# First modulation as columns: weight blocks held stationary, tokens turned in pairs, loads interleaved with the weights

## The chip, the core and the metric

The kernel runs on one core of a Trainium2 chip. The metric is device time in microseconds (us) of one launch. Engines are named as in the profile: PE is the matrix engine (PEld its weight loads), DVE the vector engine, ACT the scalar engine, POOL the GpSimd engine, SP the engine whose queue issues most DMAs. A matmul has a *stationary* operand, which a weight load puts into PE's array, and a *moving* operand, which is then streamed through it column by column.

## The reference, cut to what matters

One layer of a diffusion backbone with 1024 latent and 256 context tokens of width 1024. The part that the change touches is the first modulation, which everything else reads:

```python
mod_l = silu(c) @ w_ada + b_ada          # c: (1, 1024); w_ada: (1024, 6144)
mod_c = silu(c_ctx) @ w_ada + b_ada      # the context tokens have a vector of their own
sh1, sc1, g1, sh2, sc2, g2 = split(mod_l, 6)
hl = rmsnorm(x,   norm1_w) * (1 + sc1)  + sh1      # 8 tiles of 128 tokens
hc = rmsnorm(ctx, norm1_w) * (1 + csc1) + csh1     # 2 tiles of 128 tokens
y  = token_mix(hc, hl, ...)              # in-projection, 8 heads of mLSTM and retention, out-projection
xl = x + g1 * y
out = rmsnorm(xl + g2 * expert_choice_ffn(rmsnorm(xl) * (1 + sc2) + sh2))
```

All of it is float32. Of `w_ada`, the first 2048 columns (shift and scale, 8 MB) are needed before any projection can start.

## The kernel before, in words

The precise products go as two or three passes of a float32 form that PE takes in one pass each (`F32R`): a value is split into `hi` and `lo = value - hi`, and `hi*hi + hi*lo + lo*hi` is summed. A plain float32 matmul stands in the trace as two passes.

**The start.** `ccol` (both condition vectors, 8 blocks of 128 rows by 2) gives `sig = silu(ccol)`. The 8 MB of `w_ada` come as eight tiles `wa` of 1 MB (three buffers, line 222). Each of the four blocks of 512 modulation columns takes two tiles. In blocks 0 and 2 the kernel multiplies in plain float32 (line 271): `sig` (2 columns) is stationary, the weights move, 512 columns at a time. In blocks 1 and 3 the weights are first split by ACT and DVE (lines 275, 276), and the passes go in `F32R` (line 278), with a stationary tile `cst` of 128 columns. The result is a row of 512 values for both vectors in PSUM (`prow`); ACT copies it out (line 282) and four small matmuls (line 284) turn it into columns of `mps`, 128 partitions by 2.

**The tokens.** `norm_x` squares a tile of 128 tokens (ACT or DVE, lines 239, 237), POOL makes the inverse root (lines 128, 129) and DVE (tiles 0 to 5) or POOL (tiles 6 to 9, line 245) scales it. Then for each of three groups (context: tiles 0, 1; latent: 2 to 5; 6 to 9) and each of 8 blocks of 128 features, PE transposes the block of each token tile into `pt` (line 328), ACT applies scale and shift (`full`, line 330) and DVE makes `hh` and `hl` of it (lines 331, 332). Before them `b1` and `a1` (lines 302 to 304) are made of `mps`.

**The first head.** Its in-projection weights come as two tiles of 1 MB in the buffers of `wa`, are split by ACT and by DVE and POOL in turn (lines 179, 180), and `gemm` (line 355) multiplies `hh` and `hl` of a token tile with them, 24 passes for each tile. `gates` (lines 382, 387) does the same with 16 gate columns. `prep` makes keys, values and states of a token tile.

**Order.** The DMAs of the start are pinned in program order on SP's queue. On the other engines the recording layer orders instructions; each engine works through its own list in order, and an instruction that waits holds up what stands behind it on that engine. A tile's buffer comes free when its last reader is done. After the start come eight heads, the out-projection with the router, and sixteen experts whose weights stream from memory. The start is the only place that the change touches.

Of the kernel before, what the change touches and what calls it, by code (L numbers as in the profile page):

```python
# [71 lines left out]
def _pack(i):  # L72
# [15 lines left out]
    o["wada1"] = cont(wa[:, :2 * D].reshape(2, 4, 128, 4, 512).transpose(3, 0, 2, 1, 4))  # L88
# [30 lines left out]
def build(tc, A, out):  # L119
# [95 lines left out]

    early = ExitStack()
    ep = early.enter_context(tc.tile_pool(name="early", bufs=1))
    eps_ = early.enter_context(tc.tile_pool(name="early_ps", bufs=1, space=PSUM))
# [5 lines left out]
    def load_x(tt):  # L224
        if tt == 8:
            xts[8], xts[9] = (lambda a: (a[:, 0], a[:, 1]))(
                ep.tile([128, 4, 512], F32, name="wa", bufs=3).rearrange("p (a b) c -> p a (b c)", a=2))
        xt = xts[tt] if tt >= 8 else ep.tile([128, D], F32, name="xt", bufs=6)
        pinned(xt, A["ctx"][tt] if tt < NTC else A["x"][tt - NTC])
        xts[tt] = xt  # L230

    def norm_x(tt):
        xt = xts[tt]
        sq = ep.tile([128, D], BF16, name="sq")
        ss = ep.tile([128, 1], F32, name="ss", bufs=3)
        if tt % 2 and tt > 2:
            V.scalar_tensor_tensor(sq, xt, 1.0, xt, op0=ALU.mult, op1=ALU.mult, accum_out=ss)
        else:
            S.activation(sq, xt, AF.Square, accum_out=ss)
        r = ep.tile([128, 1], F32, name="r", bufs=3)  # L240
        rsqrt_mean(r, ss, D, ep)
        if tt < 6:
            V.tensor_scalar(xt, xt, r, None, op0=ALU.mult)
        else:
            G.tensor_scalar(xt, xt, r, 1.0, op0=ALU.mult, op1=ALU.mult)
# [7 lines left out]
    cst = ep.tile([128, 4 * KD + 128], F32R, name="cst")  # L253
    cs4 = cst[:, 0:4 * KD].rearrange("p (k s j) -> p k s j", s=2, j=2)
    V.tensor_copy(cst[:, 4 * KD:], ident)
    V.tensor_copy(cs4[:, :, :, 0], sig)
    V.tensor_tensor(cs4[:, :, :, 1], sig, cs4[:, :, :, 0].bitcast(F32), op=ALU.subtract)
    sel = ep.tile([4, 2], F32, name="sel")
    V.tensor_tensor(sel, ident[0:4, 0:4:2], ident[0:4, 1:4:2], op=ALU.add)

    ret_decay()
    mps = eps_.tile([128, 16, 2], F32, name="mps")
    for b in range(4):
        prow = eps_.tile([128, 512], F32, name="prow", bufs=2)
        for g in range(2):
            wa = ep.tile([128, 4, 512], F32, name="wa", bufs=3)
            pinned(wa, A["wada1"][b, g])
            for j in range(4):
                k = 4 * g + j
                if b % 2 == 0:  # L270
                    PE.matmul(prow[0:2], lhsT=sig[:, k], rhs=wa[:, j], start=(k == 0), stop=(k == 7))  # L271
                    continue
                wh = wp.tile([128, 512], F32R, name="whi")
                wl = wp.tile([128, 512], F32R, name="wlo")
                S.copy(wh, wa[:, j])
                V.tensor_tensor(wl, wa[:, j], wh.bitcast(F32), op=ALU.subtract)
                for q, w in enumerate((wh, wl)):
                    PE.matmul(prow, lhsT=cst[:, 4 * k:4 * k + 128], rhs=w, start=(k == 0 and q == 0),
                              stop=(k == 7 and q == 1))
        nr = 2 if b % 2 == 0 else 4  # L280
        rows = ep.tile([128, 512], F32, name="full", bufs=3)[0:nr]
        S.copy(rows, prow[0:nr])
        for j in range(4):
            PE.matmul(mps[:, 4 * b + j], lhsT=rows[:, j * 128:(j + 1) * 128],
                      rhs=sel if nr == 4 else ident[0:2, 0:2], start=True, stop=True)
    for tt in groups[0]:
        load_x(tt)
        norm_x(tt)
    wcur = [], []
    for q in range(2):  # L290
        wa = ep.tile([128, 4, 512], F32, name="wa", bufs=3)
        pinned(wa.rearrange("p (a b) c -> p a b c", a=2),
               A["win"][HEADS[0], 2 * q:2 * q + 2].rearrange("a p b c -> p a b c"))
        for j in range(4):
            split_w(wa[:, j], wcur, G if j % 2 else V)
    for tt in groups[1]:
        load_x(tt)
        norm_x(tt)
# [8 lines left out]
    pinned(wg, A["wmg"])  # L307
    wgt = cp.tile([128, 32 * KD + 96], F32R, name="wgs")
    wgs = wgt[:, 0:32 * KD].rearrange("p (k c) -> p k c", k=KD)
    for tt in groups[2]:  # L310
        load_x(tt)
    first = [pinned(kpre, A["k_pre"])]
# [5 lines left out]
    for gi, grp in enumerate(groups):  # L318
        if gi == 2:
            for tt in grp:  # L320
                norm_x(tt)
        n = 128 * len(grp)
        hh, hl = hT[gi]
        w = 1 if gi == 0 else 0
        for k in range(KD):
            pt = eps_.tile([128, 512], F32, name="pt", bufs=3)
            for j, tt in enumerate(grp):
                PE.transpose(pt[:, j * 128:(j + 1) * 128], xts[tt][:, k * 128:(k + 1) * 128], ident)
            full = ep.tile([128, 512], F32, name="full", bufs=3)
            S.activation(full[:, :n], pt[:, :n], AF.Identity, bias=b1[:, k, w:w + 1], scale=a1[:, k, w:w + 1])  # L330
            V.tensor_copy(hh[:, k], full[:, :n])  # L331
# [996 lines left out]
```

## Time and profile before

| | us |
|---|---|
| three runs: median (lowest to highest) | 2330.57 (2322.81 to 2331.26) |
| the profiled execution | 2328.49 |
| its span, first to last instruction | 2326.7 |
| first pass on PE | 8.48 |
| `mps` complete (36.39 + 1.05) | 37.44 |
| first pass of the in-projection | 41.55 |
| in-projection of the fourth token tile starts | 77.25 |
| PE gets over its wait for the first `qk` | 86.95 |

The mean granted clock of PE over the span is 0.987 of full speed; full is 2.4 GHz, half is 1.2 GHz. The start that the change touches is the first 4% of the span.

How to read the rows below: a line of a timeline is *start, duration, engine, line, operation, out<-in, shapes, count, [idle before it <- what ended that]*, with several equal instructions in one line. For PE, `128*2 128x512` is stationary partitions and columns, then moving partitions by columns. Durations on PE run from a pass's start to its end and overlap with the next pass; the distance from one start to the next is what a pass costs in a stream.

### The profile page before, as it was taken

What the parts mean: (1) busy time and instruction counts of PE and PEld (TensorE: products, weight loads), DVE (VectorE), ACT (ScalarE), POOL (GpSimd) and SP (SyncE); (2) the same over time, 40 slices, a digit from 0 to 9 for tenths busy, and PEclk for the clock granted to TensorE, in tenths of its full rate; (3) what the DMA queues carried; (4) which work ended last, traced back from release to release, by engine and by line L of the source; (5) the groups of instructions that cost most, each with busy time, mean ns of one, the idle gap of its engine ahead of it and who ended that gap; (6) DMA issues with size and microseconds to landing.
All of it is one profiled execution on the core that took longest, in us unless ns stands there. A gap on an engine that the chain in (4) does not pass through costs nothing.

```text
span 2326.7 us, 31080 instructions
## 1 busy us (share of the span) xinstructions
PE 2255.3 (97%) x11270; PEld 1851.0 (80%) x11270; DVE 1788.6 (77%) x2092; ACT 1415.9 (61%) x1812; POOL 385.4 (17%) x724
## 2 busy tenths in 40 slices
PE   7999999999997899999999999999999999999997
PEld 4788888888786677888888888888888888888886
DVE  5554545655556989888888888988888889888887
ACT  5433434222434566777777677677776777777775
POOL 2444445444411000000000000000000000000004
PEclk8999999999998999999999999999999999999999
DMA  7123322233474879999999999999999999999995
GB/s 283 53 60 105 109 71 81 87 107 127 136 270 168 323 287 348 365 380 380 362 383 357 381 376 363 382 366 376 375 364 381 365 375 374 364 387 357 376 396 230
DMA packets 133390, 664.68 MB, mean 286 GB/s; under 512 B 14221, under 2 KB 44021, under 8 KB 64629
## 3 DMA queue, kind: packets, MB, share of 16 engines
q1 hardware_dynamic: 126181, 635.78, 72.2%
q0 software_dynamic: 6768, 24.83, 3.8%
q8 instruction: 88, 1.44, 0.2%
q10 hardware_dynamic: 288, 2.10, 0.2%
q14 instruction: 65, 0.53, 0.1%
HBM read 637.50 MB, written 25.15 MB: 285 GB/s over the span
## 4 chain that ended last, share of the span: by engine, by line
PE 82%; DMA 6%; DVE 5%; ACT 2%; issue 2%; POOL 2%; SPq 0%; POOLq 0%; ACTq 0%; DVEq 0%
PE w_gate L976 20%; PE w_up L976 20%; PE y L976 20%; PE g L355 10%; DMA raw<-in_wada 3%; PE y L741 3%; PE T L976 3%; DVE lo L976 2%; DMA raw<-in_win 1%; PE U L573 1%; PE prow L271 1%; POOL r L129 1%; DVE raw L668 1%; ACT hi L976 1%; PE O L621 1%
## 5 line engine op out<-in xcount | busy, mean ns | idle before, releaser
L976 DVE TENSOR_TENSOR lo<-raw,hi 128x2048 fp32r<-128x2048 f32 x528 | 1185.2, 2286 | 134.5 <-ACT hi L976 122.3
L976 ACT CAST hi<-raw 128x2048 fp32r<-128x2048 f32 x528 | 971.6, 1903 | 0.9 <-DVE xl L976 0.6
L976 PE MATMUL w_gate<-hi,xh 128*128 128x512 f32 (+1 forms) x768 | 298.7, 389 | 0.1
L976 PE MATMUL w_gate<-hi,xl 128*128 128x512 f32 (+1 forms) x768 | 291.3, 379 | 0.0
L976 PE MATMUL w_gate<-lo,xh 128*128 128x512 f32 (+1 forms) x768 | 290.5, 378 | 0.0
L976 PE MATMUL w_up<-hi,xl 128*128 128x512 f32 (+1 forms) x768 | 289.6, 377 | 0.0
L976 PE MATMUL w_up<-lo,xh 128*128 128x512 f32 (+1 forms) x768 | 288.9, 376 | 0.5 <-DVE lo L976 0.5
L976 PE MATMUL w_up<-hi,xh 128*128 128x512 f32 (+1 forms) x768 | 288.4, 376 | 0.0
L976 ACT CAST th<-T 128x512 fp32r<-128x512 f32 x96 | 53.0, 552 | 330.8 <-PE T L976 330.8
L355 PE MATMUL g<-whi,hh 128*128 128x512 f32 (+1 forms) x640 | 248.2, 388 | 4.0 <-DVE hh L331 2.1
L355 PE MATMUL g<-whi,hl 128*128 128x512 f32 (+1 forms) x640 | 246.0, 384 | 1.3 <-DVE hl L332 1.2
L355 PE MATMUL g<-wlo,hh 128*128 128x512 f32 (+1 forms) x640 | 243.6, 381 | 0.0
L976 PE MATMUL y<-lo,th 128*128 128x512 f32 x704 | 226.6, 395 | 0.7 <-DVE lo L976 0.7
L976 PE MATMUL y<-hi,th 128*128 128x512 f32 x704 | 226.8, 396 | 0.5 <-ACT th L976 0.5
L976 PE MATMUL y<-hi,tl 128*128 128x512 f32 x704 | 226.2, 395 | 0.0
L1227 POOL DMA_INDIRECT acc_d<-yo,idx x15 | 23.8, 1588 | 889.2 <-DVE yo L976 889.2
L976 PEld LDWEIGHTS w_gate<-hi,xl 128*128 128x128 f32 x768 | 145.4, 189 | 29.2
L976 PEld LDWEIGHTS w_up<-lo,xh 128*128 128x128 f32 x768 | 144.1, 188 | 30.8 <-DVE lo L976 1.1
L976 PEld LDWEIGHTS w_up<-hi,xh 128*128 128x128 f32 x768 | 144.5, 188 | 28.7
L976 PEld LDWEIGHTS w_gate<-lo,xh 128*128 128x128 f32 x768 | 145.8, 190 | 26.5
L976 PEld LDWEIGHTS w_up<-hi,xl 128*128 128x128 f32 x768 | 144.2, 188 | 28.4
L976 PEld LDWEIGHTS w_gate<-hi,xh 128*128 128x128 f32 x768 | 145.8, 190 | 26.2 <-ACT xh L976 0.5
(376 smaller groups left out, 3196.9 us busy)
## 6 DMA issues: line engine op xcount, KB each, us to landing
raw<-in_w_up SPq DMA_DIRECT2D x176, 1024.0 KB, 7.3
raw<-in_w_down SPq DMA_DIRECT2D x176, 1024.0 KB, 7.2
raw<-in_w_gate SPq DMA_DIRECT2D x174, 1024.0 KB, 7.2
raw<-in_wada SPq DMA_DIRECT2D x32, 512.0 KB, 4.4
raw<-in_win SPq DMA_DIRECT2D x28, 512.0 KB, 3.7
wa<-in_wada SPq DMA_DIRECT2D x8, 1024.0 KB, 4.9
xt<-in_x SPq DMA_DIRECT2D x14, 512.0 KB, 7.8
aux<-in_k_rope SPq DMA_DIRECT2D x32, 128.0 KB, 2.1
```

Of the source, the lines that this page charges most:

```text
L129: G.tensor_tensor(dst, m, mhalf, op=ALU.pow)
L271: PE.matmul(prow[0:2], lhsT=sig[:, k], rhs=wa[:, j], start=(k == 0), stop=(k == 7))
L355: PE.matmul(dst, lhsT=a[:, k], rhs=w[:, c0:512], start=(k == 0 and q == 0), stop=(k == 7 and q == 2))
L573: PE.matmul(pU[:, dr], lhsT=kw[:, dr], rhs=v[:, 0:NV], start=True, stop=True)
L621: PE.matmul(pO[:, dr], lhsT=k1[:, dr], rhs=v, start=True, stop=True)
L668: V.scalar_tensor_tensor(raw, raw, 1.0, crow, op0=ALU.mult, op1=ALU.mult, accum_out=mcol[:, n:n + 1])
L741: PE.matmul(y, lhsT=a[:, k], rhs=w[:, k], start=(k == 0 and q == 0), stop=(k == 7 and q == 2))
L976: return lambda *a, **k: tc.keep_in_program_order(f(*a, **k))
L1227: nc.gpsimd.indirect_dma_start(out=acc_d, out_offset=bass.IndirectOffsetOnAxis(ap=idx[:, :1], axis=0), in_=yo, in_offset=None, compute_op= ...
```

## The change

The modulation is now computed straight as columns. `w_ada` is packed into eight tiles of 256 modulation columns, each with the full depth of 1024 rows. For every 128 of these columns the weight block is the stationary operand (128 by 128, plain float32) and `sig` (2 columns) moves; eight such matmuls sum one column block of `mps`. `prow`, the split of `w_ada`, `cst`, `sel`, the copies and the turning are gone.

The loads are reordered on SP: the context tokens stand behind the sixth tile of weights, and the four quarters of the first head's weights around the eighth, each in a buffer of its own (`raw`, two buffers). Seven buffers `xt` hold token tiles. All splits of the first head go to DVE, and all ten scalings of tokens too (POOL keeps the inverse root).

The tokens are turned two tiles at a time instead of four: for each pair and each two feature blocks, four transposes into one PSUM tile (`O` and `I` in turn), two ACT instructions of 256 columns, one cast `hh` of 512 columns (DVE and ACT in turn) and one subtraction on DVE. The PSUM pools of the later stage are opened before the start and the start uses their tiles.

```diff
-    o["wada1"] = cont(wa[:, :2 * D].reshape(2, 4, 128, 4, 512).transpose(3, 0, 2, 1, 4))
+    o["wada1"] = cont(wa[:, :2 * D].reshape(KD, 128, 8, 256).transpose(2, 1, 0, 3).reshape(8, 128, 2048))
...
-        if tt < 6:
-            V.tensor_scalar(xt, xt, r, None, op0=ALU.mult)
-        else:
-            G.tensor_scalar(xt, xt, r, 1.0, op0=ALU.mult, op1=ALU.mult)
+        V.tensor_scalar(xt, xt, r, None, op0=ALU.mult)
...
-    mps = eps_.tile([128, 16, 2], F32, name="mps")
-    for b in range(4):
-        prow = eps_.tile([128, 512], F32, name="prow", bufs=2)
-        for g in range(2):
-            wa = ep.tile([128, 4, 512], F32, name="wa", bufs=3)
-            pinned(wa, A["wada1"][b, g])
-            for j in range(4):
-                k = 4 * g + j
-                if b % 2 == 0:
-                    PE.matmul(prow[0:2], lhsT=sig[:, k], rhs=wa[:, j], start=(k == 0), stop=(k == 7))
-                    continue
...
+    mps = psu.tile([128, 16, 2], F32, name="S")
+    raws = []
+    for t in range(8):
+        wa = ep.tile([128, KD, 256], F32, name="wa", bufs=3)
+        pinned(wa, A["wada1"][t].rearrange("p (k c) -> p k c", k=KD))
+        for c in range(2):
+            for k in range(KD):
+                PE.matmul(mps[:, 2 * t + c], lhsT=wa[:, k, c * 128:(c + 1) * 128], rhs=sig[:, k],
+                          start=(k == 0), stop=(k == 7))
+        if t == 5:
+            for tt in (0, 1):
+                load_x(tt)
+                norm_x(tt)
+        if t >= 6:
+            for q in (2 * t - 12, 2 * t - 11):
+                raws.append(wp.tile([128, 2, 512], F32, name="raw", bufs=2))
+                pinned(raws[-1], A["win"][HEADS[0], q])
+                if q == 0:
+                    wcur = [], []
+                for j in range(2):
+                    split_w(raws[-1][:, j], wcur, V)
+    for tt in range(2, 6):
         load_x(tt)
+    first = [pinned(kpre, A["k_pre"])]
+    for tt in range(6, NTT):
         load_x(tt)
...
-        for k in range(KD):
-            pt = eps_.tile([128, 512], F32, name="pt", bufs=3)
...
+    for t0 in range(0, NTT, 2):
+        if t0:
+            norm_x(t0)
+            norm_x(t0 + 1)
...
+        for kk in range(KD // 2):
+            pt = ps.tile([128, 2, 256], F32, name="OI"[kk % 2])
+            for j in range(2):
+                k = 2 * kk + j
+                for tt in range(2):
+                    PE.transpose(pt[:, j, tt * 128:(tt + 1) * 128], xts[t0 + tt][:, k * 128:(k + 1) * 128], ident)
+            full = ep.tile([128, 2, 256], F32, name="full", bufs=3)
+            for j in range(2):
+                k = 2 * kk + j
+                S.activation(full[:, j], pt[:, j], AF.Identity, bias=b1[:, k, w:w + 1], scale=a1[:, k, w:w + 1])
+            sl = slice(2 * kk, 2 * kk + 2)
+            (V.tensor_copy if kk % 2 == 0 else S.copy)(hh[:, sl], full)
+            V.tensor_tensor(hl[:, sl], full, hh[:, sl].bitcast(F32), op=ALU.subtract)
```

What this moves, by the lists of instructions. On PE, the last of the modulation before (`prow` the row, `mps` the columns, `pt` the transposed tokens, `g` the in-projection; numbers tell buffers apart):

```order
L278 MATMUL prow_223<-whi_270,cst_105 128x512
L278 MATMUL prow_223<-wlo_271,cst_105 128x512
L328 MATMUL pt_394<-ident_64,xt_282 128x128
L328 MATMUL pt_401<-ident_64,xt_282 128x128
L328 MATMUL pt_408<-ident_64,xt_282 128x128
L284 MATMUL mps_125<-sel_109,full_276 128x2 x4
L328 MATMUL pt_394<-ident_64,xt_292 128x128
```

The same place now, from the first pass on (`S` holds the modulation columns, `wa` the weight tiles):

```order
L257 MATMUL S_125<-sig_107,wa_126 128x2 x16
L257 MATMUL S_125<-sig_107,wa_144 128x2 x16
L257 MATMUL S_125<-sig_107,wa_162 128x2 x16
L257 MATMUL S_125<-sig_107,wa_180 128x2 x16
L257 MATMUL S_125<-sig_107,wa_198 128x2 x16
L257 MATMUL S_125<-sig_107,wa_216 128x2 x16
L257 MATMUL S_125<-sig_107,wa_254 128x2 x16
L257 MATMUL S_125<-sig_107,wa_292 128x2 x16
L305 MATMUL O_355<-ident_64,xt_234 128x128
```

Eight groups of sixteen matmuls with a moving operand of 2 columns, nothing between them, take the place of 48 matmuls of 512 columns and 16 small ones; no transpose stands ahead of the last of them any more.

On SP's queue, the loads of the start before (`wa<-in_win` and `raw<-in_win` are the head's weights, `nw` and `aux` the first data of the stage behind):

```order
L222 DMA wa<-in_wada 128x2048 x8
L222 DMA xt<-in_ctx 128x1024 x2
L222 DMA wa<-in_win 128x2x1024 x2
L222 DMA xt<-in_x 128x1024 x4
L222 DMA wg<-in_wmg 128x128
L222 DMA xt<-in_x 128x1024 x2
L222 DMA wa<-in_x 128x1024 x2
L222 DMA kpre<-in_k_pre 128x1026
L523 DMA aux<-in_k_rope 128x256 x2
L473 DMA nw<-in_hnw 128x128
```

and now:

```order
L224 DMA wa<-in_wada 128x2048 x6
L224 DMA xt<-in_ctx 128x1024 x2
L224 DMA wa<-in_wada 128x2048
L224 DMA raw<-in_win 128x1024 x2
L224 DMA wa<-in_wada 128x2048
L224 DMA raw<-in_win 128x1024 x2
L224 DMA xt<-in_x 128x1024 x4
L224 DMA kpre<-in_k_pre 128x1026
L224 DMA xt<-in_x 128x1024 x4
L224 DMA wg<-in_wmg 128x128
L500 DMA aux<-in_k_rope 128x256 x2
L450 DMA nw<-in_hnw 128x128
```

The seventh and eighth weight tiles now stand behind the context tokens and half of the head's weights; the order of what the next stage reads (`aux`, `nw`) is kept.

On ACT, the start of the token stage now (the sums of squares `sq`, the head's casts `whi`, then scale and shift in pieces of 256 columns with the cast `hh` of every second one):

```order
L237 ACTIVATE sq,ss<-xt 128x1024 x2
L179 CAST whi<-raw 128x512 x8
L237 ACTIVATE sq,ss<-xt 128x1024 x3
L309 ACTIVATE full<-O,b_347,a_348 128x256 x2
L309 ACTIVATE full<-I,b_347,a_348 128x256 x2
L311 CAST hh_75<-full 128x512
L309 ACTIVATE full<-O,b_347,a_348 128x256 x2
```

Before, the casts `whi` stood among the first `full` pieces, and ACT had no `hh`; now the casts and five of the squares stand ahead of the first `full`, and half of the `hh` casts are ACT's.

## Rows read from the trace of the kernel before

**Rows 1.** Page of the profile, busy time (share) and instructions of PE.

```profile
PE 2255.3 (97%) x11270; PEld 1851.0 (80%) x11270; DVE 1788.6 (77%) x2092; ACT 1415.9 (61%) x1812; POOL 385.4 (17%) x724
```

**Rows 2.** Busy by stretch: PE, PEld, DVE, ACT, POOL, clock, DMA, GB/s.

```profile
8.48:12.20 3.72, 3.72 (x5) 0.59 (x6) 0.00 (x0) 0.04 (x1) 0.00 (x0) 1.00 1.01 425
12.20:37.44 25.24, 25.05 (x96) 11.97 (x95) 11.49 (x18) 13.60 (x25) 1.81 (x4) 1.00 0.87 325
...
39.54:53.20 13.66, 10.78 (x39) 8.28 (x39) 13.56 (x27) 8.24 (x17) 9.46 (x10) 0.50 0.62 229
...
77.25:87.33 10.08, 7.49 (x33) 5.68 (x34) 2.41 (x7) 4.78 (x16) 4.32 (x10) 1.00 0.76 208
87.33:90.74 3.41, 3.41 (x12) 2.83 (x11) 1.30 (x6) 1.30 (x6) 2.38 (x6) 0.51 0.01 2
90.74:196.00 105.26, 105.26 (x579) 89.66 (x578) 46.89 (x151) 35.22 (x124) 44.11 (x116) 1.00 0.17 49
...
624.60:626.60 2.00, 2.00 (x19) 2.00 (x19) 0.88 (x3) 0.83 (x4) 0.25 (x2) 0.99 0.35 98
626.60:630.05 3.45, 3.45 (x10) 2.61 (x10) 0.43 (x2) 0.27 (x1) 0.49 (x1) 0.51 0.09 24
```

**Rows 3.** Timeline of PE, first stage.

```profile
8.48 8.83 PE L271 MATMUL prow<-wa,sig 128*2 128x512 f32 x16 [8.48 <-DMA wa<-in_wada]
...
26.05 3.60 PE L271 MATMUL prow<-wa,sig 128*2 128x512 f32 x8
...
36.39 1.05 PE L284 MATMUL mps<-sel,full 4*128 4x2 f32 x8 [0.19 <-ACT full L282]
```

**Rows 4.** Lines of PE up to 37.4: count | busy, mean | idle.

```profile
L278 PE MATMUL prow<-whi,cst 128*128 128x512 f32 x16 | 6.6, 414 | 0.0
...
L284 PE MATMUL mps<-sel,full 4*128 4x2 f32 x16 | 2.1, 249 | 0.2 <-ACT full L282 0.2
```

**Rows 5.** Line L905, small matmuls: duration ns, first and last start.

```profile
L905 PEld LDWEIGHTS pl<-hT,mcol x16: 190/190/220, 624.6 to 626.3; 128*128 128x128 f32 x16
L905 PE MATMUL pl<-hT,mcol x16: 182/262/263, 624.7 to 626.3; 128*128 128x16 f32 x16
```

**Rows 6.** Timeline of PEld, two bursts.

```profile
41.55 0.29 PEld L355 LDWEIGHTS g<-whi,hh 128*128 128x128 f32 x1 [1.57 <-DVE hh L331]
41.71 0.34 PEld L355 LDWEIGHTS g<-wlo,hh 128*128 128x128 f32 x1
...
77.25 0.19 PEld L355 LDWEIGHTS g<-whi,hh 128*128 128x128 f32 x1 [0.66 <-ACT qk L535]
77.36 0.19 PEld L355 LDWEIGHTS g<-wlo,hh 128*128 128x128 f32 x1
77.59 0.19 PEld L355 LDWEIGHTS g<-whi,hl 128*128 128x128 f32 x1
```

**Rows 7.** Timeline of ACT, first head and first tokens.

```profile
36.99 2.17 ACT L179 CAST whi<-wa 128x512 fp32r<-128x512 f32 x4 [0.65 <-DMA wa<-in_win]
39.07 1.47 ACT L330 ACTIVATE full<-pt,b,a 128x256 f32<-128x256 f32 x3
```

**Rows 8.** Timeline of PE at half clock.

```profile
41.92 0.42 PE L355 MATMUL g<-wlo,hh 128*128 128x256 f32 x1
42.14 0.63 PE L328 MATMUL pt<-ident,xt 128*128 128x128 f32 x2
42.42 0.56 PE L355 MATMUL g<-whi,hl 128*128 128x256 f32 x1
```

**Rows 9.** Timeline of DVE, end of the token stage.

```profile
77.91 0.69 DVE L332 TENSOR_TENSOR hl<-full,hh 128x512 fp32r<-128x512 f32 x1
```

**Rows 10.** Timeline of SP, issue of `nw`.

```profile
77.94 0.44 SPq L473 DMA_DIRECT2D nw<-in_hnw  x1
```

**Rows 11.** Timeline of POOL and of PE behind it.

```profile
83.60 0.47 POOL L512 TENSOR_TENSOR o<-th,nw 128x128 f32<-128x128 f32 x1 [2.64 <-DMA nw<-in_hnw]
...
86.95 0.33 PE L544 MATMUL T<-ident,qk 128*128 128x128 f32 x1 [2.59 <-POOL qk L533]
```

More of the change, by code (lines that the diff above doesn't have):

```diff
@@ L214, in ret_decay @@
         S.activation(rdec[:, 0], lg, AF.Exp, scale=128.0)
+    pg = gps.enter_context(tc.tile_pool(name="g_ps", bufs=2, space=PSUM, side="right", reuse_waits="tile"))
+    psu = gps.enter_context(tc.tile_pool(name="su_ps", bufs=1, space=PSUM, side="right", reuse_waits="tile"))
+    ps = mix.enter_context(tc.tile_pool(name="mix_ps", bufs=1, space=PSUM, reuse_waits="tile"))
     early = ExitStack()
     ep = early.enter_context(tc.tile_pool(name="early", bufs=1))
-    eps_ = early.enter_context(tc.tile_pool(name="early_ps", bufs=1, space=PSUM))
     xts = {}
@@ L224, in load_x @@
     def load_x(tt):
[L225 to L230, printed above, removed]
+        xts[tt] = ep.tile([128, D], F32, name="xt", bufs=7)
+        pinned(xts[tt], A["ctx"][tt] if tt < NTC else A["x"][tt - NTC])
     def norm_x(tt):
@@ L252, in build @@
     V.tensor_tensor(sig, sig, ccol, op=ALU.mult)
[L253 to L259, printed above, removed]
-    ret_decay()
-    mps = eps_.tile([128, 16, 2], F32, name="mps")
@@ L263, in build @@
-    for b in range(4):
-        prow = eps_.tile([128, 512], F32, name="prow", bufs=2)
-        for g in range(2):
-            wa = ep.tile([128, 4, 512], F32, name="wa", bufs=3)
-            pinned(wa, A["wada1"][b, g])
-            for j in range(4):
-                k = 4 * g + j
-                if b % 2 == 0:
-                    PE.matmul(prow[0:2], lhsT=sig[:, k], rhs=wa[:, j], start=(k == 0), stop=(k == 7))
-                    continue
[L273 to L285, printed above, removed]
@@ L286, in build @@
-    for tt in groups[0]:
-        load_x(tt)
[L288 to L296, printed above, removed]
+    ret_decay()
+    mps = psu.tile([128, 16, 2], F32, name="S")
+    raws = []
@@ L297, in build @@
+    for tt in range(2, 6):
+        load_x(tt)
+    first = [pinned(kpre, A["k_pre"])]
+    for tt in range(6, NTT):
         load_x(tt)
-        norm_x(tt)
     b1 = ep.tile([128, KD, 2], F32, name="b1")
@@ L306, in build @@
     wg = ep.tile([128, KD, 16], F32, name="wg")
-    pinned(wg, A["wmg"])
+    first.append(pinned(wg, A["wmg"]))
     wgt = cp.tile([128, 32 * KD + 96], F32R, name="wgs")
     wgs = wgt[:, 0:32 * KD].rearrange("p (k c) -> p k c", k=KD)
-    for tt in groups[2]:
-        load_x(tt)
-    first = [pinned(kpre, A["k_pre"])]
     def behind(dst, src):
@@ L316, in behind @@
             nc.sync.dma_start(dst, src)
[L318 to L323, printed above, removed]
-        w = 1 if gi == 0 else 0
-        for k in range(KD):
-            pt = eps_.tile([128, 512], F32, name="pt", bufs=3)
[L327 to L331, printed above, removed]
-            V.tensor_tensor(hl[:, k], full[:, :n], hh[:, k].bitcast(F32), op=ALU.subtract)
+    for t0 in range(0, NTT, 2):
+        if t0:
+            norm_x(t0)
+            norm_x(t0 + 1)
+        gi = next(g for g, grp in enumerate(groups) if t0 in grp)
+        o = 128 * (t0 - groups[gi][0])
+        hh, hl = (a[:, :, o:o + 256] for a in hT[gi])
+        w = 1 if gi == 0 else 0
+        for kk in range(KD // 2):
[11 more added lines that the diff above has]
+            V.tensor_tensor(hl[:, sl], full, hh[:, sl].bitcast(F32), op=ALU.subtract)
     V.tensor_copy(wgt[:, 32 * KD:], ident[:, 0:96])
@@ L336, in build @@
     early.close()
-    pg = gps.enter_context(tc.tile_pool(name="g_ps", bufs=2, space=PSUM, side="right", reuse_waits="tile"))
-    psu = gps.enter_context(tc.tile_pool(name="su_ps", bufs=1, space=PSUM, side="right", reuse_waits="tile"))
     mp = mix.enter_context(tc.tile_pool(name="mix", bufs=2, reuse_waits="tile"))
-    ps = mix.enter_context(tc.tile_pool(name="mix_ps", bufs=1, space=PSUM, reuse_waits="tile"))
     pg_cur = [None]
```

## The prediction

> **What bounds the kernel now.** I began with the page: PE is busy for 97% of the span [rows 1], so a gain elsewhere counts only where PE waits for it. Then the busy times by stretch [rows 2], to see whether the start is different. It is: up to 37.44 PE is fully busy, from 39.54 to 53.20 it works with gaps at half clock (0.50, that is 1.2 GHz), from 77.25 to 87.33 it has gaps again, and from 90.74 to 196 it is busy for 105.26 of 105.26 us. So the start ends as a bound at about 91 us, and whatever the change saves or loses before that goes on to the end: behind it no idle time of PE is left that could take up a delay. Then the timelines of the engines that PE waits for. The start is a chain of three: the modulation (8.48 to 37.44 [rows 3]), the turning of the tokens between PE, ACT and DVE (to 78.60 on DVE [rows 9]), and a wait for `qk` that PE gets over at 86.95 [rows 11].
>
> **The modulation, removed.** It is PE work with hardly a gap. Line 271: sixteen passes in 8.8 us, then two groups of eight at 3.6 us [rows 3]. Line 278: two groups of sixteen passes [rows 4] at 0.23 us, the distance between the loads at 77.36 and 77.59 [rows 6], 7.4 us. Line 284: 32 passes [rows 4] at (1.05 - 0.25) / 7 = 0.11 us [rows 3, 4], 3.7 us. Sum 27.1 of the 28.96 us from 8.48 to 37.44. The splits of weights on ACT and DVE lay beside it.
>
> **The modulation, added.** 16 column blocks by 8 depth blocks are 128 matmuls in plain float32. Such a matmul stands in the trace as two passes: the kernel has eight of line 284 with each stationary source and rows 4 count sixteen. So 256 passes, each with a weight load of 128 columns and 2 moving columns. The moving side costs next to nothing, the weight load sets the pace. The nearest row is line 905, a plain float32 matmul with 128 by 128 stationary and 16 moving columns: sixteen passes start from 624.7 to 626.3 [rows 5], 1.6 / 15 = 0.107 us each, at a granted clock of 0.99 [rows 2]. At that price: 256 x 0.107 = 27.4 us, the modulation ends at 35.9, and nothing is won or lost there.
>
> The question is the clock. At the start it is low: the first sixteen passes of line 271 are (8.83 - 0.59) / 15 = 0.55 us apart in the mean, later eight are (3.60 - 0.59) / 7 = 0.43 apart [rows 3] (0.59 us is about one pass with its end). The column of the clock says 1.00 from 8.48 to 12.20 because its first record comes only then; the passes themselves tell that the level was the low one, and that it rose after PE had streamed 512 columns at a time for 3.7 us. What do small passes do to the clock? Rows 5 with rows 2 show the only long run of them: from 624.60 to 626.60 PE was busy for 2.00 of 2.00 us at 0.99, and in the 3.45 us behind it the granted clock was 0.51. Weight loads with little streamed behind them did not hold the clock up. I therefore expect that 256 passes of 2 columns, beginning at the low level, leave it at 1.2 GHz to their end.
>
> The Trainium skill says otherwise in "TensorE: Matmul & The Clock Gate", Part 1, "The HAM clock gate": the clock follows how busy PE has recently been, and sustained activity releases it. By that rule the busy weight loads would raise it; the rows at 624.60 speak against that reading. The rival of the full clock below is this rule's case.
>
> What does a pass cost at half clock? In a burst at 0.50 the loads at 41.55 (0.29 long) and 41.71 (0.34) end at 41.84 and 42.05, 0.21 apart; at full clock those at 77.25 and 77.36 (0.19 each) end 0.11 apart [rows 6]. So the load takes twice the time. Their starts are only 0.16 apart, the lower bound (256 x 0.16 = 41 us). I take twice 0.107, 0.214, since the ends repeat it: 256 x 0.214 = 54.8, and the modulation ends at 63.3 instead of 37.44, 25.9 us later.
>
> The Trainium skill, "TensorE: Matmul & The Clock Gate", section "LDWEIGHTS (loading the stationary operand)", gives a load's time as its columns over 1.2 without regard to the gate. By it the sum would be 27.3 us at either clock; the 0.19 against 0.29 us of rows 6 disagree.
>
> **The loads.** A tile of weights is then used up in 32 x 0.214 = 6.8 us, and 1 MB comes in 2.5 us (425 GB/s [rows 2]). The buffers, not the DMAs, pace the queue; the eighth tile waits until the fifth is used up (8.48 + 5 x 6.85 = 42.7), and what stands behind it, half of the head's weights and token tiles 2 to 6, is issued then and is in, split and scaled before 63. That costs nothing, hidden under PE's passes, and neither do the scalings and splits that DVE takes over from POOL: DVE has nothing else to do until the modulation ends. With PE at full clock this cover would be half as long and some of it would show.
>
> **The turning.** s is 63.3.
> (a) Context: 24 transposes (four pieces of the context, two of the first latent pair) and 48 passes of 256 columns up to the last pass of the context tiles, at half clock 0.21 to 0.22 each [rows 8], 72 x 0.215 = 15.5, and some 0.5 for the first wait on ACT: s + 16. Dense work brings the clock back (8.48 to 12.20, and 87.33 to 90.74 [rows 2]); with the last half of it at full speed, s + 12.
> (b) 24 passes of 512 columns at 0.23 and 16 transposes at half of 0.21: 7.2, s + 19.2. Beside it DVE takes the last token tile, whose buffer comes free only when the first latent pair is turned, and the casts behind it wait on DVE; I count nothing for that, and 2 us if the load is late.
> (c) Ten pieces are left, with nothing beside them. ACT needs per piece two instructions of 256 columns at (1.47 - 0.57) / 2 = 0.45 [rows 7] (0.57 is one alone) and every second time a cast at 2.17 / 4 = 0.54: 1.17. Before, DVE was the slow one here. 11.7 us, s + 30.9; DVE's last `hl` [rows 9] ends 0.7 later, s + 31.6 = 94.9, against 78.60.
> (d) The gate passes of the context, 16 of 256 columns at half of 0.23, 1.9: the fourth token tile starts at about s + 33 = 96.3 against 77.25 [rows 6].
> (e) `nw` is issued 0.66 us before the last `hl` ends [rows 9, 10], and PE gets over the wait for `qk` 9.0 us behind the issue [rows 10, 11]. The order of these loads is kept: 94.9 - 0.66 + 9.0 = 103.2 against 86.95, 16.3 later. The tile before it on PE takes 24 x 0.23 = 5.6, from 96.3 to 102; PE then waits 1 instead of 2.6 us, and the half clock from 87.33 to 90.74 [rows 2], 1.7 us lost, may not come.
>
> Sum: between 16.3 - 1.7 = 14.6 and 16.3; with the 2 us of (b), 18.3. I take 16: 2328.5 + 16 = 2344.5. The profiled execution is 2.1 us under the median, so 2345 against it. The forecast's own range: the clock back sooner or later in (a), and the bounds of (e), 2339 to 2351.
>
> **Rivals.** *Full clock.* If weight loads alone keep the array's clock up, it rises at about 12.2: 17 passes at 0.214, 239 at 0.107, end at 37.7. The turning then runs at full clock, and (a) shrinks to some 10 us: s + 30 = 67.7 for the last `hl`, 10.9 earlier than before; with the tokens' loads less well covered 8 to 11, so about 2320. For it: the pace of rows 5 was held at 0.99. Against: what came after it. It decides if the clock is 1.00 before 16 us. *Cheaper load.* 0.16 per pass at half clock: modulation ends at 49.5, 13.8 earlier than in the forecast, 2331: no change. For it the starts in rows 6, against it the ends. *Low clock to the end of the start.* In (c) PE works 0.44 of each 1.17 us and waits for ACT, which is thinner work than that of 39.54 to 53.20, where the clock stayed at 0.50. (a) takes 4 more, the gates and the fourth tile 7.5 more, of which the wait in (e) takes 1: 2355. *Nothing is passed on.* If some later wait took up the delay, 2329; 105.26 of 105.26 us speaks against it.
>
> **Chances.** Forecast 0.58, low clock to the end 0.13, cheaper load 0.09, full clock 0.17, nothing passed on 0.03. This kernel is told from no change at about 0.5%, 11.7 us. Slower (over 2342): 0.87 of the forecast, by its own range, and all of the low clock, 0.63. Faster (under 2319): a third of the full clock, 0.06. The same: the rest, 0.31. The range leaves out most of the full clock and a tail above: 2323 to 2355.
>
> **What would show it.** `S<-sig,wa` 256 passes, 0.21 apart, last one at about 63, granted clock 0.50 under them; `b` on DVE at 63 to 64; ACT as the engine that PE waits for between 83 and 95; the fourth token tile at about 96; the wait for `qk` near 1 us; from 110 us on the same lines at the same distances as before. Wrong would be passes 0.11 apart in the first 30 us, a clock of 1.00 there, or a `b` before 45.

## The result, and the profile after

The changed kernel takes 2350.4 us (median of 4 runs, 2346.7 to 2352.9), the kernel before in the same series 2329.4: a ratio of 1.0088, 95% interval 1.0071 to 1.0105, or 20.5 us more (16.5 to 24.5). The forecast was 2345, 16 us more, in a range from 2323 to 2355. The profiled execution of the changed kernel took 2352.9 us, the slowest of the four, with a span of 2351.2.

First the page's busy times of the changed kernel, which answer to [rows 1]:

```profile
PE 2280.7 (97%) x11430; PEld 1894.1 (81%) x11430; DVE 1774.7 (75%) x2062; ACT 1414.1 (60%) x1818; POOL 378.6 (16%) x716
```

PE is busy for 25.4 us more, its weight loads for 43.1, and DVE, ACT and POOL for less. So the loss is work of PE, or the same work more slowly done. The timeline of PE over the first stage (start, duration, engine, line, operation, count; what ended the idle time) stands against [rows 3]:

```profile
8.39 54.74 PE L257 MATMUL S<-sig,wa 128*128 128x2 f32 x256 [8.39 <-DMA wa<-in_wada]
62.99 1.09 PE L305 MATMUL O<-ident,xt 128*128 128x128 f32 x4
...
65.97 0.56 PE L332 MATMUL g<-whi,hh 128*128 128x256 f32 x1
...
73.98 0.48 PE L332 MATMUL g<-whi,hh 128*128 128x512 f32 x1
```

54.74 / 256 = 0.214 us a pass, with no gap, and the last ends at 63.13; before, the modulation ended at 37.44. The next rows are DVE's, which adds the bias and at last splits the tokens, then PE's in the turning (against [rows 6, 9]):

```profile
63.17 0.17 DVE L279 TENSOR_TENSOR b<-S,cols 128x16 f32<-128x16 f32 x1 [0.51 <-PE S L257]
...
93.64 0.69 DVE L312 TENSOR_TENSOR hl<-full,hh 128x512 fp32r<-128x512 f32 x1 [0.32 <-ACT hh L311]
```

```profile
88.34 0.65 PE L305 MATMUL I<-ident,xt 128*128 128x128 f32 x4 [0.77 <-ACT full L309]
89.25 0.65 PE L305 MATMUL O<-ident,xt 128*128 128x128 f32 x4 [0.26 <-ACT full L309]
90.68 0.67 PE L305 MATMUL I<-ident,xt 128*128 128x128 f32 x4 [0.78 <-ACT full L309]
93.02 0.58 PE L359 MATMUL I<-hh,wgs 128*128 128x256 f32 x1 [1.67 <-ACT full L309]
96.59 0.63 PE L332 MATMUL g<-whi,hh 128*128 128x512 f32 x1
```

The last `hl` ends at 94.33 instead of 78.60, and the fourth token tile starts at 96.59 instead of 77.25. In between PE waits for ACT, piece after piece. Each piece leaves PE idle for 0.26 to 0.78 us of some 1.17, and the clock falls once more. Busy time by stretch shows it (columns as in [rows 2]):

```profile
63.20:66.90 3.70, 3.44 (x16) 3.04 (x16) 1.68 (x6) 2.74 (x6) 0.00 (x0) 1.00 0.00 0
66.90:91.19 24.29, 20.27 (x138) 17.06 (x136) 18.49 (x33) 20.58 (x43) 3.91 (x6) 1.00 0.35 85
91.19:98.02 6.83, 5.16 (x22) 4.72 (x21) 3.43 (x8) 6.47 (x22) 2.57 (x6) 0.50 0.58 206
```

The clock's column says 1.00 in the first of these rows because this trace has no record of the clock ahead of 67.3 us; the passes of 256 columns, 0.41 us long at 66.33 and 0.28 from 67.47 on, tell that it was the lower level (the experiment "warm" below has a record for the modulation itself).

How far does the delay go? Three instructions of DVE, the same ones in both kernels, first before, then after:

```profile
112.55 0.28 DVE L549 COPY qTt<-T 128x128 f32<-128x128 f32 x1
335.54 0.35 DVE L597 SCALAR_TENSOR_TENSOR st<-st,dec,U 128x130 f32<-128x130 f32 x1 [1.59 <-PE U L573]
860.57 2.29 DVE L976 TENSOR_TENSOR lo<-raw,hi 128x2048 fp32r<-128x2048 f32 x1
```

```profile
128.02 0.28 DVE L526 COPY qTt<-T 128x128 f32<-128x128 f32 x1
351.45 0.35 DVE L574 SCALAR_TENSOR_TENSOR st<-st,dec,U 128x130 f32<-128x130 f32 x1 [1.59 <-PE U L550]
884.84 2.28 DVE L953 TENSOR_TENSOR lo<-raw,hi 128x2048 fp32r<-128x2048 f32 x1
```

15.5 us late at 112, 15.9 at 335, 24.3 at 860, and the same to the end. So the start costs 15.5 us, close to the forecast, and 8.4 us of this pair of executions arise between 335 and 860 us, where nothing was expected and where both kernels issue the same instructions but for a few exchanged neighbours.

### The profile page after: what moved, and what is told of

The parts are those of the page before. It is cut to its first block, busy times and chain, and to the rows that moved or that the text cites. A ratio compares the mean times of both kernels' runs of the same rounds, so it can differ in the third digit from the quotient of the medians.

```text
span 2351.2 us, 31362 instructions
## 1 busy us (share of the span) xinstructions
PE 2280.7 (97%) x11430; PEld 1894.1 (81%) x11430; DVE 1774.7 (75%) x2062; ACT 1414.1 (60%) x1818; POOL 378.6 (16%) x716
## 4 chain that ended last, share of the span: by engine, by line
PE 83%; DMA 6%; DVE 4%; ACT 3%; issue 2%; POOL 1%; SPq 0%; POOLq 0%; ACTq 0%; DVEq 0%
PE w_gate L953 20%; PE y L953 20%; PE w_up L953 20%; PE g L332 11%; PE T L953 3%; DMA raw<-in_wada 2%; PE S L257 2%; PE y L718 2%; DVE lo L953 1%; DMA raw<-in_win 1%; PE U L550 1%; DMA zr<-zt_d 1%; DVE raw L645 1%; ACT hi L953 1%; PE O L598 1%
## 5 line engine op out<-in xcount | busy, mean ns | idle before, releaser
L953 PEld LDWEIGHTS w_up<-lo,xh 128*128 128x128 f32 x768 | 144.2, 188 | 30.8 <-DVE lo L953 1.1
## 6 DMA issues: line engine op xcount, KB each, us to landing
aux<-in_k_rope SPq DMA_DIRECT2D x32, 128.0 KB, 2.1
```

The source lines that it names most:

```text
L953: return lambda *a, **k: tc.keep_in_program_order(f(*a, **k))
```

## The experiments

Theory: a modulation pass is bound by its weight load; the load takes twice the time at 1.2 GHz; and the clock stays there while almost nothing streams. Rivals: a float32 load costs 0.21 us at any clock; busy loads keep a full clock; or the loss comes from the rest of the change.

The table holds all runs. "Start" is the time of the `qTt` instruction of the rows above, "distance" the time from it to the `lo` instruction, and "low" the time at 1.2 GHz in between, both worked out from the one profiled execution of each kernel. Ratios are to the kernel before, with 95% intervals.

| kernel | median us | ratio | start | distance | low |
|---|---|---|---|---|---|
| before | 2326 to 2329 | | 112.6 | 748.0 | 34.1 |
| changed | 2350.4 | 1.0088 (1.0071 to 1.0105) | 128.0 | 756.8 | 44.4 |
| wide (e1_wide) | 2331.8 | 1.0018 (1.0009 to 1.0027) | 112.1 | 752.4 | 41.0 |
| warm (e2_warm) | 2339.0 | 1.0046 (1.0032 to 1.0059) | 126.5 | 749.8 | 34.1 |
| rows (e3_rows) | 2332.0 | 1.0016 (1.0006 to 1.0027) | 114.3 | 753.4 | 37.5 |
| columns only (e4_cols_only) | 2347.3 | 1.0084 (1.0071 to 1.0097) | 128.0 | 753.4 | 41.0 |
| 3.4 us longer (p1_longer) | 2346.9 | 1.0089 (1.0074 to 1.0104) | 132.2 | 743.5 | 30.7 |
| 6.9 us longer (p2_longer) | 2353.6 | 1.0099 (1.0082 to 1.0116) | 135.5 | 753.5 | 41.0 |
| 10.3 us longer (p3_longer) | 2356.2 | 1.0114 (1.0097 to 1.0131) | 137.8 | 749.8 | 37.5 |
| wide, PE held (f1_hold) | 2326.6 | 0.9998 (0.9987 to 1.0009) | 111.4 | 750.4 | 37.5 |
| wide, fours (f2_fours) | 2332.9 | 1.0026 (1.0014 to 1.0037) | 112.4 | 755.2 | 44.4 |
| wide, fours, held (g1_fours_hold) | 2333.3 | 1.0030 (1.0017 to 1.0042) | 114.8 | 751.0 | 34.1 |
| before, held (h1_before_hold) | 2330.3 | 1.0005 (0.9993 to 1.0018) | 109.0 | 753.9 | 44.4 |
| wide, warm, held (k1_warm_hold) | 2328.4 | 0.9996 (0.9984 to 1.0007) | 108.6 | 751.9 | 41.0 |

**Wide.** The same loads, 128 moving columns instead of 2:

```diff
-    PE.matmul(mps[:, 2 * t + c], lhsT=wa[:, k, c * 128:(c + 1) * 128], rhs=sig[:, k],
+    PE.matmul(mpw[t // 2][:, 2 * (t % 2) + c].rearrange("p (r j) -> p r j", j=2),
+              lhsT=wa[:, k, c * 128:(c + 1) * 128], rhs=sig[:, k, None].broadcast_to([128, 64, 2]),
```

> The changed kernel with 128 moving columns in each pass of the modulation instead of 2 (each of the two columns repeated 64 times, the outputs in four PSUM banks); the same 128 weight blocks are loaded, and columns 0 and 1 are read. Theory: the 0.214 us of a pass are a weight load at the lower clock, and the clock is low because almost no columns stream; with 128 columns the granted clock rises during the modulation, passes fall to about 0.107 us, the 256 passes end at 36 to 42 us instead of 63.1, and the time falls by 18 to 24 us against the changed kernel (2326 to 2332). Rival: a load of an f32 weight block costs 0.21 us whatever the clock and whatever streams; then the passes stay at 0.214 or go above, they end at 63 or later, and the time stays within 3 us of the changed kernel's.

Timeline of PE in the first stage of this kernel:

```profile
8.45 9.43 PE L258 MATMUL S<-sig,wa 128*128 128x128 f32 x64 [8.45 <-DMA wa<-in_wada]
17.71 7.31 PE L258 MATMUL U<-sig,wa 128*128 128x128 f32 x64
24.86 7.31 PE L258 MATMUL g<-sig,wa 128*128 128x128 f32 x64
...
33.52 7.53 PE L258 MATMUL g<-sig,wa 128*128 128x128 f32 x64
45.86 1.12 PE L308 MATMUL O<-ident,xt 128*128 128x128 f32 x4 [4.81 <-ACT full L312]
```

Sixty-four times as many columns, and a pass takes about half the time: (24.86 - 17.71) / 64 = 0.112 us behind the first twenty, which still are 0.213 apart. The modulation ends at 41.05 and the time falls to 2331.8. That a load costs 0.21 us at any clock is refuted.

**Warm.** Dense work ahead of the modulation, which keeps its 2 columns:

```diff
+    wps = pg.tile([128, 512], F32, name="g")
+    for _ in range(20):
+        PE.matmul(wps, lhsT=wm[:, 0:128], rhs=wm, start=True, stop=True)
     mps = psu.tile([128, 16, 2], F32, name="S")
```

> The changed kernel with 20 bf16 matmuls of 512 columns on a zeroed tile ahead of the modulation, which is left at 2 columns a pass. Theory: the clock is full when the first weights land, and falls again while the passes run, since they stream almost nothing; they start at 0.107 us and go back to 0.214, the last ends at 57 to 62 us, and the time falls by 1 to 6 us against the changed kernel. Rival: back-to-back weight loads keep a full clock once it is there; then the passes end at 36 to 40 us and the time falls by 18 to 25 us.

The modulation's line by stretch in this kernel (length, PE and PEld busy with their counts, clock, DMA share, GB/s), cut where the record of the clock changes:

```profile
8.30:11.17 2.87, 2.87 (x26) 2.87 (x27) 1.00 0.99 420
11.17:60.43 49.26, 49.26 (x232) 49.17 (x231) 0.50 0.66 243
```

Both prices in one run, for the same 2-column passes: 2.87 / 26 = 0.11 us at 1.00 and 49.26 / 232 = 0.21 at 0.50. The clock fell at 11.17 although PE was busy without a gap for the 2.87 us ahead of the fall and for 49 us after it. In this run busy weight loads with 2 columns behind them did not keep it. The rival by the Trainium skill's rule, "TensorE: Matmul & The Clock Gate", Part 1, "The HAM clock gate", by which activity releases the throttle, is refuted for these passes; the 1.00 of "wide" agrees with it. The start came 1.5 us earlier, as expected; the time fell by more than the 1 to 6 us forecast (11.5 between the medians). In the two profiled executions the distance behind the start is 7.0 shorter, which the forecast had no term for. More on that below.

**Rows.** Only the modulation put back, on the new tiles of weights:

```diff
-        for c in range(2):
-            for k in range(KD):
-                PE.matmul(mps[:, 2 * t + c], lhsT=wa[:, k, c * 128:(c + 1) * 128], rhs=sig[:, k],
+        for k in range(KD):
+            if t % 4 < 2:
+                PE.matmul(prow[0:2], lhsT=sig[:, k], rhs=wa[:, k], start=(k == 0), stop=(k == 7))
+                continue
...
```

> The changed kernel with only the modulation put back to rows (weights as the moving operand, 256 columns a matmul, half of the tiles split into high and low parts as in the kernel before, then turned into columns by small matmuls); its loads between the weights, its tiles of whole depth and the turning in pairs stay. Theory: the modulation is the whole loss and the rest of the change is a gain of about 9 us: the modulation ends at 37 to 40 us, and the time is 2316 to 2328, 22 to 32 below the changed kernel and 2 to 14 below the kernel before. Rival: the turning in pairs, bound by ScalarE at 1.17 us a piece, loses by itself; then the time stays at or above the kernel before's.

The time is 2332.0, as the rival has it, but not for its reason. From ACT's and PE's timelines:

```profile
36.30 2.54 ACT L269 CAST whi<-wa 128x256 fp32r<-128x256 f32 x8
40.38 1.14 ACT L179 CAST whi<-raw 128x512 fp32r<-128x512 f32 x2 [1.54 <-DMA raw<-in_win]
41.78 1.14 ACT L179 CAST whi<-raw 128x512 fp32r<-128x512 f32 x2 [0.27 <-DMA raw<-in_win]
42.83 0.36 ACT L276 COPY full<-g 4x256 f32<-4x256 f32 x1
```

```profile
43.24 0.82 PE L278 MATMUL S<-sel,full 4*128 4x2 f32 x4 [3.01 <-ACT full L276]
```

The copy that the last step of the modulation needs stands on ACT behind the head's weights, which wait for their loads; the modulation ends at 44.05, not at 37 to 40. From there the turning is quick: the last `hl` ends 35.5 us after the modulation, against 41.2 in the kernel before. So it isn't the stage behind the modulation that loses: it is 5.7 us shorter, and the modulation, which ends 6.6 us later on these loads, takes them back. That the turning in pairs makes it shorter is not shown by this run; the next one bears on it.

**Columns only.** The kernel before with the column modulation alone:

```diff
-        prow = eps_.tile([128, 512], F32, name="prow", bufs=2)
-        for g in range(2):
...
+        for c in range(2):
+            for k in range(KD):
+                PE.matmul(mps[:, 2 * t + c], lhsT=wa[:, k, c * 128:(c + 1) * 128], rhs=sig[:, k],
```

> The kernel before with only the modulation as columns (and the weight tiles of whole depth that it needs); its loads, its turning in fours and its PSUM tiles stay. Theory: the modulation ends at 63 us as in the changed kernel, 25.7 later than before, and since nothing of the rest is shorter the start ends 18 to 26 us late: 2347 to 2358. Rival: the kernel before has slack behind its modulation that takes up the delay, and the loss of the changed kernel comes from the turning in pairs and the new order of loads; then the time is within 8 us of the kernel before's.

The modulation ends at 63.0 and the start is at 128.0, as in the changed kernel; the time is 2347.3. The modulation by itself brings the whole loss. The last split of this kernel:

```profile
96.78 1.29 DVE L309 TENSOR_TENSOR hl<-full,hh 128x512 fp32r<-128x512 f32 x2
```

It ends 35.1 us behind the modulation, against 41.2 in the kernel before and 31.2 in the changed kernel. So the old turning, too, is 6 us shorter behind a later modulation. One difference that the traces show is that ACT is through with the head's casts at 63.3, where in the kernel before they went on to 42.6, 5 us behind the modulation; that this makes the 6 us is not shown. The other 3.9 us come with the new turning and loads, but nothing of them is left at the start; from 91.19 to 98.02, where the changed kernel works at 0.50, this one has 1.00.

**Longer by 3.4, 6.9 and 10.3 us.** The changed kernel, its last column block computed two, three and four times. On every engine the order of the instructions is that of the changed kernel:

```diff
-        for c in range(2):
+        for c in range(2) if t < 7 else (0, 1, 1):
```

> The changed kernel with its last column block of the modulation computed twice: 16 more passes at 0.214 us, 3.4 us more of the same work, nothing else. Theory A (what comes after the start is the same work, moved): the modulation ends at 66.5 us instead of 63.1 and the time grows by 3.4 us, to 2351 to 2357. Theory B (the stretch from 340 to 800 us costs more or less according to when it begins, since the granted clock falls there in some places; the runs so far lost between -3 and +6 us there against the kernel before with one and the same instructions): the start ends 3.4 us later and the time moves by something else, between -5 and +8.

> The changed kernel with the last column block of its modulation computed three times: 32 passes more, 6.9 us, every engine's order of work the same. Theory A: what follows is the same work, moved; the start ends 6.9 us later than in the changed kernel and the time is 6.9 above it, 2357. Theory B (the stretch from 340 to 800 us costs more or less by when it begins): the start ends 6.9 us later and the time does not follow it: 2350 to 2363, with low-clock stretches after 300 us of another length than in the changed kernel's trace and in that of 3.4 us more.

> The same with the block computed four times: 48 passes more, 10.3 us. Theory A: 2361, 10.3 above the changed kernel. Theory B: 2353 to 2367, not on one line with 0, 3.4 and 6.9 us more; the time follows the length of the low-clock stretches after 300 us in each trace.

The starts follow: 4.1, 7.5 and 9.8 later than in the changed kernel. The times follow less plainly: 3.4 us more work leaves the ratio at 1.0089, and in the profiled pair the kernel with more work is 9 us faster. But that pair is the slowest of four runs of the changed kernel and the fastest of five of the longer one, and either ratio is known to 3.5 to 4 us. The three DVE instructions of the longer one:

```profile
132.16 0.28 DVE L526 COPY qTt<-T 128x128 f32<-128x128 f32 x1
354.23 0.35 DVE L574 SCALAR_TENSOR_TENSOR st<-st,dec,U 128x130 f32<-128x130 f32 x1 [1.58 <-PE U L550]
875.67 2.28 DVE L953 TENSOR_TENSOR lo<-raw,hi 128x2048 fp32r<-128x2048 f32 x1
```

The first four stretches at 0.50 behind the start of the changed kernel, and, in the second fence, the first one of the kernel longer by 3.4 us:

```profile
367.67:371.08 3.41, 2.92 (x7) 2.34 (x8) 2.65 (x8) 1.30 (x7) 2.84 (x5) 0.50 0.62 175
647.60:651.00 3.40, 3.40 (x9) 2.53 (x9) 0.43 (x2) 0.27 (x1) 0.42 (x1) 0.50 0.07 19
691.90:698.75 6.85, 5.13 (x14) 4.21 (x15) 3.78 (x13) 3.74 (x9) 2.21 (x6) 0.50 0.31 103
756.80:777.30 20.50, 9.11 (x43) 7.17 (x44) 12.60 (x29) 11.51 (x17) 3.07 (x2) 0.50 0.29 96
```

```profile
747.60:768.10 20.50, 9.15 (x42) 7.32 (x43) 12.66 (x29) 11.45 (x18) 3.17 (x3) 0.50 0.28 98
```

The changed kernel loses the clock at three places ahead of 757 us where the longer one keeps it. In both, PE has the same list of passes in this stretch. Pass against pass, about 5 of the 13.3 us between the two distances arise at passes inside these three places, and 5.6 in four waits of PE that are longer in the changed kernel (one of them in the third place). Another of the four, first in the changed kernel, then at the same place in the longer one:

```profile
364.04 1.23 DVE L645 SCALAR_TENSOR_TENSOR raw<-raw,crow 128x1024 f32<-128x1024 f32 x1 [2.25 <-DMA raw<-in_wada]
366.02 0.46 PE L532 MATMUL S<-k,kT 128*128 128x128 f32 x2 [1.56 <-DVE k L540]
```

```profile
365.39 1.23 DVE L645 SCALAR_TENSOR_TENSOR raw<-raw,crow 128x1024 f32<-128x1024 f32 x1 [0.77 <-DMA raw<-in_wada]
367.37 0.46 PE L532 MATMUL S<-k,kT 128*128 128x128 f32 x2
```

`k`, which PE needs, stands behind line 645 on DVE, and line 645 waits for a load. Measured against PE's passes, that load came 1.4 us later in the changed kernel, and the clock of the changed kernel falls at 367.67, behind this wait.

Over the table the distance goes with the low time: 743.5 at 30.7, 748 to 751 at 34.1, 754 to 757 at 44.4. But a pass at 0.50 takes about twice as long (the two prices of "warm"), so 13.7 us more at the lower clock can cost some 6.9 us at most, half of the 13.3. So one and the same work costs 743 to 757 us there, in part by the clock and in part by waits for loads. Whether that hangs on when the stretch begins (theory B) or differs from one execution to the next is not shown. Each distance is a single execution, and the kernel before, in one series of 23 runs, took from 2321.3 us (mean granted clock 0.989) to 2333.6 (0.985). The times alone do not exclude theory A either: over the kernel before it expects 23.9, 27.4 and 30.8 us, where 17.2 to 24.2, 19.1 to 27.0 and 22.6 to 30.5 were measured, and the 20.5 us that it starts from are known to 4.

**Held.** PE kept at work in the gaps of the wide kernel:

```diff
+    hold(18, wa[:, 7, 128:256], ident)
...
+            if t0 >= 6:
+                hold(3, done[-2][:, 0:128], done[-2])
```

> The kernel with 128 moving columns in the modulation, and TensorE kept at work where it waits: 18 f32 matmuls of 128 columns into an unused bank behind the modulation (where it waits 4.8 us), and 3 matmuls of 256 columns behind each piece of the last four token tiles (where it waits 0.7 us a piece). Theory: what the wide modulation does not win is lost to the clock, which stood at 1.2 GHz from 43.5 to 53.7 and from 70.8 to 81.0 us with work waiting; with the clock kept, the gates and the first products behind the pieces run in half the time, the start ends 3 to 6 us earlier, and the time is 2323 to 2329. Rival: ScalarE and the loads bound those stretches, so the clock there costs nothing; then the time is within 2 us of the wide kernel's (2330 to 2334).

The number came, 2326.6, the mechanism only in part. Busy by stretch of the wide kernel, then of this one:

```profile
43.46:53.70 10.24, 6.84 (x29) 6.00 (x30) 8.65 (x17) 9.04 (x19) 7.22 (x10) 0.50 0.75 290
70.77:81.01 10.24, 8.28 (x34) 6.68 (x35) 7.28 (x15) 10.21 (x30) 0.86 (x3) 0.50 0.52 141
```

```profile
43.46:53.70 10.24, 7.20 (x48) 6.33 (x47) 8.38 (x16) 9.44 (x19) 6.11 (x8) 0.88 0.80 315
70.77:81.01 10.24, 8.67 (x60) 6.96 (x59) 7.68 (x16) 10.21 (x28) 0.55 (x2) 1.00 0.51 142
```

The clock is back, but the start is only 0.7 us earlier, not 3 to 6: in the second stretch ACT is busy for 10.21 of 10.24 us in both, and sets the pace of the pieces at either clock. What else the ratio gained (1.0018 to 0.9998) arose behind the start, where nothing was forecast; that the number fits is luck.

**Fours, fours held, before held, all three.** Eight tiles turned four at a time; PE held in that version; PE held in the kernel before; and dense work ahead of the held wide kernel:

```diff
+                S.activation(full, pt, AF.Identity, bias=b1[:, k, 0:1], scale=a1[:, k, 0:1])
```

> The kernel with 128 moving columns in the modulation, and the eight token tiles turned four at a time, one ScalarE instruction of 512 columns per piece in place of two of 256 (1.45 us for two pieces against 1.02 for one, from the kernel before and the changed one); the context pair stays. Theory: the pieces are bound by ScalarE (1.17 us each in pairs, about 0.96 so), the last hl is 2 to 4 us earlier, and the time falls by 2 to 4 us against the wide kernel, to 2327 to 2330. Rival: turning in fours waits for all four tiles, whose loads come last, and gives back what the instructions save; then the time is that of the wide kernel or above it (2331 to 2336).

> Both edits on the wide modulation: eight token tiles turned four at a time, 18 matmuls behind the modulation and 2 of 256 columns behind each piece of the last group that keep TensorE at work. Theory: the two gains add up, the start ends 6 to 9 us before that of the wide kernel, and the time is 2320 to 2326, below the kernel before. Rival: one of the two covers the other (loads of the token tiles bound both); then the time is 2326 to 2332.

> The kernel before (rows, turning in fours) with 16 f32 matmuls of 128 columns into unused columns behind its modulation and 8 of 256 columns ahead of the last token group. Theory: the kernel before loses to the clock as well (1.2 GHz from 39.5 to 53.1 us with products waiting); kept at work, the start ends 2 to 5 us earlier and the time falls to 2321 to 2326. Rival: VectorE and the loads bound that stretch, so the clock costs nothing there, and the matmuls added stand ahead of the first products; then the time is within 2 us of the kernel before's, or above.

> The kernel with the wide modulation and TensorE kept at work behind it, with 40 bf16 matmuls of 256 columns on a zeroed tile ahead of the modulation too. Theory: the modulation begins at 2.4 GHz instead of 1.2 (its first passes were 0.21 us until about 13.5 us), its last pass is 1.5 to 2.5 us earlier, as far as the loads of the weights let it, and the time is 1 to 3 us below the kernel without them, about 2324 to 2326. Rival: the loads set the end of the modulation, and the time is the same (2326 to 2328).

Fours missed, and the rival is right: PE waits for the last tile, and ACT with it.

```profile
71.01 0.47 PE L304 MATMUL O<-ident,xt 128*128 128x128 f32 x1 [3.24 <-DVE xt L240]
```

With PE held it is no better, above the range of both its theories. The kernel before, held, gained 3.6 us in the start and, in the profiled executions, lost 5.9 in the distance behind it: no change. So the start moved as its theory had it, and the time is its rival's. The last version has the earliest start of all, 4.0 us ahead of the kernel before, with its modulation at full clock from the first pass and ending at 39.33; behind it the distance gives back 3.9, and its ratio is 0.9996 (0.9984 to 1.0007). The earlier end of the modulation came as its theory had it, the time of 2324 to 2326 did not. No version beats the kernel before by what can be measured; the changed kernel is beaten by 16 to 19 us (from the ratios and from the medians) with 128 columns in place of 2.

## Why the prediction was right, and where it was wrong

- **The modulation**, 256 passes at 0.214, end at 63.3: right (0.214, 63.13), and for the reason given. The step drawn from the 3.45 us behind line 905 [rows 2, 5], that small passes do not hold the clock, is shown by "warm"; the doubled load, taken from the ends in [rows 6] and not from the starts, by the two prices in the same run. At full clock a pass is 0.112, not 0.107.
- **The loads**, hidden under the passes: right; the eighth tile is issued at 42.68, forecast 42.7. "Rows" and "wide" show that with a shorter modulation they are not; there the head's weights come last.
- **(a)** s + 12: a little long. The first product of a latent tile alone (512 columns) starts at 73.98, s + 10.9. The clock came back at 67.3.
- **(b), (c)** Right in place and price. PE waits for ACT from 82 to 93, 1.17 us a piece, and the last `hl` ends at 94.33 instead of 94.9.
- **(d)** 96.3 forecast, 96.59 measured, by two errors that nearly cancel, which is luck: the gate passes began at 93.02, 1.4 us ahead of where the sum had them (96.3 less 1.9), and took 3.6 us instead of 1.9, since the clock fell at 91.19 and they ran at half clock, 0.21 each instead of 0.115. That is the beginning of the rival "low clock to the end".
- **(e)** This step failed in its mechanism. I let `nw` be issued 0.66 us before the last `hl` ends, and that fixed the wait for `qk`. The changed kernel issues it 6.9 us before that end, and the wait is gone:

```profile
87.43 0.43 SPq L450 DMA_DIRECT2D nw<-in_hnw  x1
```

```profile
95.04 0.30 POOL L488 TENSOR_SCALAR th<-th 128x128 f32<-128x128 f32 x1 [13.35 <-DMA nw<-in_hnw]
...
98.96 0.74 POOL L510 TENSOR_TENSOR qk<-t,t 128x256 f32<-128x256 f32 x1
```

(The first row names the load as what came last; DVE's `th`, which POOL needs as well, ended at 94.95 and is what released it.) `qk` is done at 99.7, and PE reaches its `T<-ident,qk` at 103.63 with no gap ahead of it. That is where (e) put it, 103.2, because the gates and the fourth tile fill the time, at 1.2 GHz up to 98.02: PE's work has replaced the wait, and that the number fits is luck. The distance of a load to its consumer was taken over from a trace in which that load happened to be issued last.
- **"From 110 us on the same distances"** failed: in the profiled pair 15.5 became 24.3 between 112 and 885 us. The sum has no term for it. In the ratios it is some 5 us (20.5 less 15.5), with the interval 1 to 9. The instructions behind the start are the same, so it isn't work that the change adds. Nor is it there in every kernel with a late start: "warm" starts 14 us late and loses 10.7 (7.5 to 13.7). Whether the 5 us belong to the moment at which that stretch begins or to the single executions stays open.
- **The rivals.** Full clock: refuted by "warm" as a thing that happens by itself, and its price was too good: 2320 forecast for the full clock, 2331.8 where 128 columns bring it. Its modulation ends at 41.05 instead of 37.7, and PE then waits 4.8 us behind the head's weights on ACT, where the sum charged at most 3 us for loads less well covered. Cheaper load: refuted, 0.21. Nothing passed on: of the 25.7 us that the modulation ends later, 15.5 arrive, since the stage behind it is shorter by 10. "Columns only" shows that this isn't owed to the turning in pairs: with the old turning as many arrive.

## What to carry to other kernels

A matmul with a few moving columns is priced by its weight load, and at whichever level the clock stands; before turning a product into such passes, ask what will have streamed on PE just before and during them. If they cannot be avoided, repeating the moving columns up to the width of the block (128 here) left a pass at 0.112 us and brought the clock back. And when a delay is carried to the end over a long stretch with some idle time in it, count the forecast's width from how much that stretch varies by itself: here 13 us between single executions, as large as most of the terms of the sum.

## What the runs showed of the hardware that was not expected

- PE can be busy for 49.26 of 49.26 us and be granted 0.50 throughout; 128 moving columns instead of 2, with the same loads, bring 1.00.
- A plain float32 pass of 128 by 128 takes 0.112 us at full clock with 2 or with 128 moving columns, and 0.214 at half clock.
- One and the same list of passes took PE 743.5 us and 756.8 us in two executions. Some 5 us of that lie in stretches at 1.2 GHz and 5.6 in four waits, one of them behind a load that DVE waited for.
- With PE held at work from 70.77 to 81.01 us the granted clock went from 0.50 to 1.00, and the start came 0.7 us earlier, since ACT was busy for 10.21 of the 10.24 us.
